# Where q is turned in mixer B, which PSUM banks its pools get, and when the last norm's products are issued: a three-part change to a hybrid encoder trunk

## The chip, the core and the metric

The kernel runs on one core of one Trainium2 chip. The metric is device microseconds (us) of one execution. The names used for the engines are: PE for TensorE's matrix products, PEld for its weight loads, ACT for ScalarE, DVE for VectorE, POOL for GpSimd, SP for SyncE, which issues most transfers. Each engine takes its instructions in program order.

## The reference, cut to what matters

The trunk has two layers on 1024 tokens of width 1024. Layer 0 uses mixer A (neighbourhood attention on a grid), layer 1 mixer B. Each layer then adds a gated embedding, and one RMS norm ends the trunk.

```python
def mixer_b(h, w_in, q_norm_g, k_norm_g, w_out):
    # h: (1, 1024, 1024); 16 query heads, 4 key/value heads, head size 64
    proj = h @ w_in
    q, k, v, gate = jnp.split(proj, [1024, 1024 + 256, 1024 + 512], axis=-1)
    q = rms_norm(heads(q, 16), q_norm_g)
    k = rms_norm(heads(k, 4), k_norm_g)
    q, k = axial_rope(q), axial_rope(k)
    # four query heads share one key/value head
    sc = einsum('bkgqd,bksd->bkgqs', q_block, k) * scale
    pr = softmax(sc)
    o = einsum('bkgqs,bksd->bkgqd', pr, v)
    return (o * silu(gate)) @ w_out

def reference(x, p, ...):
    for i in range(2):
        h = rms_norm(x, norm_g[i])
        x = x + (mixer_a if i == 0 else mixer_b)(h, ...)
        g = sigmoid(rms_norm(x, ple_norm_g[i]) @ ple_w_gate[i])
        x = x + g * (p[i] @ ple_w_proj[i])
    return rms_norm(x, final_norm_g)
```

## The kernel before

Each operand of a product is split into a high part (rounded to the fp32r format) and a low part (the rest), and a product is the sum of three PE passes: high by high, high by low, low by high. A name that ends in `h` or `A` is a high part, one that ends in `l` or `B` a low one.

The kernel runs in stages: mixer A, `dense_phase(0)` (output projection of layer 0 and its gated embedding), mixer B (from about 707 to 1340 us), and `dense_phase(1)` (the same for layer 1, and the last norm). The order of the instructions on each engine is the order in which the code writes them; semaphores that the framework derives from tiles and their buffers do the rest.

Mixer B's attention is a list of 128 steps `n`, each for a query head `h`, a half `hf` of the tokens and a block `t` of 128 queries. One step has these parts:

- `f_S`: four PE products `s<-KA,QS` and `s<-KB,QS` put the scores of 128 queries against 1024 keys into a tile `s` of two PSUM banks, and DVE takes a row minimum `mn<-s` (L1211).
- `f_E`: ACT computes `P<-s,mn`, the exponential (L1217).
- `f_T`: eight PE transposes `t<-ident,P` (L1227) fill two PSUM tiles of the pool `psT`, which has two buffers; ACT copies each to `PTh` (L1229), and DVE subtracts for `PTl` (L1230). A psT buffer is free for its next user only after these readers.
- `f_AV`, once for two steps: eight products `o<-PTh,V` and then eight `o<-PTl,V`.

`q_stack` makes the queries of the heads that come next: four PE transposes `t<-ident,qt` (L1181) into one more psT tile, an ACT copy `th<-t` (L1183), and then, some ticks later, the high and low parts `QS<-th` on ACT (L1190) and DVE (L1191). It runs 16 times, 15 of them in the attention.

`mix(att, dense)` interleaves this list with projections that fill PE (`dense` items: `d<-wh,HTh` and its kind; they make the gate, the next q, k and v), one item whenever the share of work done says so. In it a queued call of `q_stack` waits in `after`, an `Evac` list, and is run after the next dense item.

[...] In mixer B the pools were opened in the order `pd` (one bank, bank 0), `psS` (scores, banks 1 to 4), `psT` (5 and 6), `psO` (7). At mixer B's entry `dalloc` and `qalloc` hand out `pd` and `psO` in turn for the first projections. What `dense_phase(1)` allocates takes these banks over afterwards: its first product tile `Y[0]` lies in bank 0.

In `dense_phase(1)` the last norm needs `X*gain` for one half of the columns; POOL makes it, tile after tile (L1706), after ACT has squared the tile (L1701).

Of the kernel before, what the change touches and what calls it, by code (L numbers as in the profile page):

```python
# [11 lines left out]
F32 = mybir.dt.float32  # L12
# [6 lines left out]
PSUM = bass.MemoryType.PSUM  # L19
# [18 lines left out]
DT = (5, 2)  # L38
FIN = (4, 4)
HOLD = 2  # L40
WARM = (8, 8)
THIRDS = {0: ((0, 1, 2), (0, 2, 1)), 1: ((0, 1, 2), (0, 1, 2))}
DP = 1
# [115 lines left out]
def trunk(ctx, tc, x, wts, rpb, gains, hgains, mask, rope, gain0, out):  # L159
# [156 lines left out]
    def mm(ps, a, b, first, last):  # L316
        pe.matmul(ps, a, b, start=first, stop=last, skip_group_check=True)  # L317
# [41 lines left out]
            while self.left:  # L359
                self.left.pop(0)()  # L360

    leave, after = Evac(), Evac()
    after.wait = True

    def mix(att, dense, lead=0, hold=0):
        for f, _ in dense[:lead]:
            f()
            pulse()
        kept = dense[len(dense) - hold:]
        dense = list(dense[lead:len(dense) - hold])  # L370
        total = sum(c for _, c in dense)
        span = sum(c for _, c in att)
        spent = done = 0.0
        since = True
        for i, (f, c) in enumerate(att):
            kind = getattr(f, "kind", None)
            if kind == "apart" and not since and (dense or len(kept) > 2):
                d, e = (dense or kept).pop(0)
                d()
                spent += e  # L380
                after.run()
            if kind in ("apart", "blocks"):
                since = False
            f()
            leave.run()
            pulse()
            done += c
            while dense and spent < total * done / span - 1e-6:
                leave.run()
                leave.wait = i + 1 < len(att) and getattr(att[i + 1][0], "first", False)  # L390
                d, c = dense.pop(0)
                d()
                leave.wait = False
                spent += c
                since = True
                after.run()
        leave.run()
        after.run()
        for f, _ in dense + kept:
            f()  # L400
            pulse()
# [598 lines left out]
    def mixer_b(pend):  # L1000
        with ExitStack() as es:
# [2 lines left out]
            kp = es.enter_context(tc.tile_pool(name="kp", bufs=3))  # L1004
            one = es.enter_context(tc.tile_pool(name="bone", bufs=1))
            sb = es.enter_context(tc.tile_pool(name="bsb", bufs=2))
            pd = es.enter_context(tc.tile_pool(name="bpd", bufs=1, space=PSUM))
            psS = es.enter_context(tc.tile_pool(name="bps", bufs=2, space=PSUM))
            psT = es.enter_context(tc.tile_pool(name="bpt", bufs=2, space=PSUM))
            psO = es.enter_context(tc.tile_pool(name="bpo", bufs=1, space=PSUM))  # L1010

# [3 lines left out]
            def dalloc():  # L1015
                if pro[0]:
                    pro[1] += 1
                    if pro[1] % 2 == 0:
                        return psO.tile([128, 512], F32, name="o")
                return pd.tile([128, 512], F32, name="d")  # L1020

            gg, ylive = {}, {}
            KA, KB, V, QT, QST, P, RS, OP = {}, {}, {}, {}, {}, {}, {}, {}
            later = Later()

            pro = [False, 0]

            def qalloc():
                pro[1] += 1
                if pro[0] and pro[1] % 2 == 0:  # L1030
                    return psO.tile([128, 512], F32, name="o")[:, :256]
                return pd.tile([128, 512], F32, name="d")[:, :256]

            def rope_in(dst, raw, tab, eng):
                nh = raw.shape[1] // 64
# [140 lines left out]
            def q_stack(pair, hf):  # L1176
                g = pair // 2
                ps = psT.tile([128, 4, 128], F32, name="t")
                c = slice((pair % 2) * 128, (pair % 2) * 128 + 128)
                for t in range(4):  # L1180
                    pe.transpose(ps[:, t], QT[g, hf][:, t, c], ident)  # L1181
                raw = sb.tile([128, 512], F32, name="th")
                act.activation(raw, ps.rearrange("p t c -> p (t c)"), AF.Copy)  # L1183
                for j in range(2):
                    own, oth = slice(64 * j, 64 * j + 64), slice(64 - 64 * j, 128 - 64 * j)
                    qs = sb.tile([128, 512], F32R, name="QS", bufs=3)
                    QST[2 * pair + j, hf] = qs

                    def high(qs=qs, own=own, oth=oth):
                        act.activation(qs[own], raw[own], AF.Copy)  # L1190
                        post.add(DQ, lambda: dve.tensor_tensor(qs[oth], raw[own], qs[own], ALU.subtract))  # L1191
                    if pro[0]:
                        high()
                    else:
                        post.add(QO[j], high)
# [39 lines left out]
            def f_AV(h, hf, t):  # L1235
                if t == 1:
                    OP[h, hf] = psO.tile([128, 512], F32, name="o")
                o = OP[h, hf][:, (t - 1) * 128:(t + 1) * 128]
                for k in range(NT):
                    mm(o, V[h // 4][:, k], PTh[:, k], t == 1 and k == 0, False)  # L1240
                for k in range(NT):
                    mm(o, V[h // 4][:, k], PTl[:, k], False, t == 3 and k == NT - 1)
                if t == 3:
                    fin = head_end(sb, h, hf, RS[h, hf], OP.pop((h, hf)), ylive, 1, gg, talloc)
                    if fin:
                        later.add(FIN[1], fin)
# [29 lines left out]
            for g in range(4):  # L1276
                att = []
                for n in range(32 * g, 32 * g + 32):
                    h, hf, t = steps[n]
                    av = n >= 2 and n % 2 == 0  # L1280
                    w = CB if av else CN
                    def turn():
                        if WQ.gate:
                            WQ.gate = False
                        later.tick()
                    att.append((turn, w[0]))
                    if av:
                        att.append((lambda n=n: f_AV(*steps[n - 1]), w[1]))
                    te = [(blocks(n), w[2])]
                    if n + 1 < len(steps):  # L1290
                        te.append((exps(n + 1), w[3]))
                    if n % 2 == 0 and n > 0:
                        te.reverse()
                    att += te
                    if n + 2 < len(steps):
                        def scores(n=n):
                            f_S(*steps[n + 2])
                            WQ.gate = n % 2 == 1 if n < 112 else None
                        att.append((scores, w[4]))
                    m = n + QS_AT  # L1300
                    if m % 8 == 0 and m < len(steps):
                        hn, fn, _ = steps[m]
                        att.append((lambda hn=hn, fn=fn: after(lambda: q_stack(hn // 2, fn)), 0.0))
                    if YLOAD_B <= n < YLOAD_B + NT:
                        att.append((lambda t=n - YLOAD_B: load_y(1, t), 0.0))
                if g == 3:
                    att.append((lambda: f_AV(*steps[-1]), CB[1]))
                def gates(p):
                    return [i for hf in range(2) for i in gate_items("bg", p, hf, dalloc, sb, gg)]
                dense = []  # L1310
                if g > 0:
                    dense += left
                if g < 3:
                    qi = q_items(g + 1, pool)
                    kv = kv_items(1, pool) if g == 1 else [None, None]
                    dense += kv[:-2] + qi[:KS] + [k for k in kv[-2:-1] if k] + qi[KS:8] + [k for k in kv[-1:] if k] + gates(2 * g + 1) + qi[8:]
                    left = gates(2 * g + 2)
                else:
                    WQ.cap[3] = 2
                    dense += gates(2 * g + 1) + pp_items(1, dalloc, sb, TAGS_B)  # L1320
                mix(att, dense, hold=HOLD + 1 if g == 3 else 0)
# [185 lines left out]
    def dense_phase(l):  # L1507
        with ExitStack() as es:
# [9 lines left out]
            pend = []  # L1518
# [83 lines left out]
            for kind in ("ple",):  # L1602
                final = l == 1
                sq = sb.tile([128, 2, NT], F32, name="sq")
                due = []
                gt = g2
                for hf in range(2):
# [69 lines left out]
                    for t, i in order:  # L1677
# [22 lines left out]
                        if hf == 0:  # L1700
                            act.activation(junk[:, cs], X[t][:, cs], AF.Square, accum_out=sq[:, 0, t:t + 1])  # L1701
                            if final:
                                due.append(t)
                            while due and n >= 17:
                                u = due.pop(0)
                                pool.tensor_tensor(X[u][:, cs], X[u][:, cs], gt[:, cs], ALU.mult)  # L1706
                            continue
# [70 lines left out]
```

## Time and profile before

| | |
|---|---|
| median of 3 runs | 1526.33 us (1525.96 to 1526.63) |
| the profiled execution | 1525.28 us, of which its span is 1523.4 us |
| granted TensorE clock | 0.997 |
| PE busy | 1496.9 us, 98% of the span |
| DVE, ACT, POOL busy | 1096.4 us (72%), 899.8 us (59%), 303.8 us (20%) |
| PE's products of mixer B's q turns (L1181) | 64 transposes, 10.1 us busy |
| ACT's copies of them (L1183) | 16, 9.4 us busy |

A row of a timeline has the start in us from the start of the span, the duration, the engine, the line of the code, the operation, the tiles it writes and reads (`out<-in`), and in brackets the idle time of the engine just before it with what ended it. Several like instructions in a row are one row (`x4`). A row of groups ends with busy time and mean ns of one, and then the idle time ahead of the group. Matmuls overlap: the next begins before the last one's end, so PE's time is best read from start to start.

### The profile page before, as it was taken

The page shows a single profiled execution, that of the slowest core. Times are in us where ns is not written, and L with a number is a line of the kernel's source. Part 1 is how long each engine was busy: PE and PEld are TensorE (multiplying, and loading weights), DVE is VectorE, ACT ScalarE, POOL GpSimd, SP SyncE. Part 2 cuts the span into 40 slices and gives each one's busy share as a digit, 9 for nine tenths or more (in the row PEclk, how much of TensorE's full clock was granted, in tenths as well). Part 3 has the DMA queues.
Part 4 walks back from the last instruction along what each step waited for, and adds up shares of the span by engine and source line. Part 5 has one row for each costly group of instructions (what it writes and reads, how often), then busy time and mean ns, then how long its engine had stood idle before and what let it go on. Part 6 is the DMA issues. An engine that isn't in the chain of part 4 may idle for free.

```text
span 1523.4 us, 24376 instructions
## 1 busy us (share of the span) xinstructions
PE 1496.9 (98%) x8976; PEld 1314.9 (86%) x8976; DVE 1096.4 (72%) x2091; ACT 899.8 (59%) x1801; POOL 303.8 (20%) x413
## 2 busy tenths in 40 slices
PE   8999999999999999999999999999999999999997
PEld 8888988988988888888998999989999888878786
DVE  7566576377477599767888786777877777789856
ACT  6565465366466635443467776666767777744432
POOL 1222232133112000010222222443131300000022
PEclk9999999999999999999999999999999999999999
DMA  8325255263121963262210111111111122763123
GB/s 255 120 98 139 82 144 163 63 157 93 36 87 56 345 249 97 83 196 93 75 50 22 32 45 50 40 32 54 47 31 45 38 76 68 237 228 115 66 88 134
DMA packets 91096, 157.22 MB, mean 103 GB/s; under 512 B 18144, under 2 KB 54112, under 8 KB 90464
## 3 DMA queue, kind: packets, MB, share of 16 engines
q1 hardware_dynamic: 85824, 139.66, 27.9%
q0 software_dynamic: 2560, 8.39, 3.1%
q10 hardware_dynamic: 2592, 7.61, 1.4%
q8 instruction: 71, 1.16, 0.3%
q14 instruction: 49, 0.40, 0.1%
HBM read 125.10 MB, written 50.83 MB: 115 GB/s over the span
## 4 chain that ended last, share of the span: by engine, by line
PE 43%; DVE 6%; ACT 2%; issue 1%; DMA 0%; POOL 0%; ACTq 0%; DVEq 0%; POOLq 0%
PE d L317 19%; PE o L317 9%; PE s L317 7%; PE t L1227 7%; PE t L317 1%; DVE xn L1560 1%; DVE PTl L1230 1%; DVE X L1456 0%; PE t L1181 0%; DVE wl L231 0%; DVE mn L1211 0%; DVE HTl L482 0%; DVE HTl L1402 0%; ACT PTh L1229 0%; ACT th L1183 0%
## 5 line engine op out<-in xcount | busy, mean ns | idle before, releaser
L317 PE MATMUL d<-wh,HTh 128*128 128x256 f32 (+1 forms) x1032 | 342.5, 334 | 3.9 <-ACT HTh L481 1.6
L317 PE MATMUL d<-wh,HTl 128*128 128x256 f32 (+1 forms) x1032 | 338.0, 329 | 0.3 <-DVE HTl L482 0.3
L317 PE MATMUL d<-wl,HTh 128*128 128x256 f32 (+1 forms) x1032 | 336.7, 328 | 0.0
L1230 DVE TENSOR_TENSOR PTl<-t,PTh 128x512 fp32r<-128x512 f32 x256 | 165.1, 684 | 108.7 <-ACT PTh L1229 107.5
L317 PEld LDWEIGHTS d<-wh,HTh 128*128 128x128 f32 x1032 | 194.8, 190 | 24.5 <-ACT HTh L481 2.0
L317 PEld LDWEIGHTS d<-wl,HTh 128*128 128x128 f32 x1032 | 194.7, 190 | 19.3
L317 PEld LDWEIGHTS d<-wh,HTl 128*128 128x128 f32 x1032 | 194.9, 190 | 18.8 <-DVE HTl L482 0.5
L317 PE MATMUL d<-HTh,wh 128*128 128x512 f32 x504 | 205.2, 407 | 0.0
L317 PE MATMUL d<-HTh,wl 128*128 128x512 f32 x504 | 198.2, 393 | 0.0
L317 PE MATMUL d<-HTl,wh 128*128 128x512 f32 x504 | 197.3, 392 | 0.0
L1217 ACT ACTIVATE P<-s,mn 128x1024 f32<-128x1024 f32 x128 | 142.8, 1116 | 51.8 <-DVE mn L1211 50.9
L1229 ACT ACTIVATE PTh<-t 128x512 fp32r<-128x512 f32 x256 | 139.9, 594 | 52.8 <-PE t L1227 52.0
L1211 DVE TENSOR_REDUCE mn<-s 128x1 f32<-128x1024 f32 x128 | 154.7, 1209 | 11.2 <-PE s L317 11.0
L1227 PE MATMUL t<-ident,P 128*128 128x128 f32 x1024 | 136.4, 274 | 5.2 <-ACT th L1183 2.9
L317 PE MATMUL s<-KA,QS 128*128 128x512 f32 (+2 forms) x384 | 134.5, 404 | 0.0
L1227 PEld LDWEIGHTS t<-ident,P 128*128 128x128 f32 x1024 | 115.2, 140 | 16.6 <-DVE PTl L1230 6.7
L231 DVE TENSOR_TENSOR wl<-wstage,wh 128x1024 fp32r<-128x1024 f32 x78 | 100.3, 1290 | 34.9 <-ACT wh L226 34.4
L317 PE MATMUL s<-KB,QS 128*128 128x512 f32 (+2 forms) x384 | 121.6, 371 | 0.0
L775 DVE TENSOR_TENSOR PTl<-t,PTh 128x384 fp32r<-128x384 f32 (+1 forms) x128 | 66.6, 520 | 75.4 <-ACT PTh L774 74.0
L317 PE MATMUL o<-PTh,V 128*128 128x256 f32 (+2 forms) x672 | 118.5, 287 | 1.2 <-DVE Y L496 0.8
L317 PE MATMUL o<-PTl,V 128*128 128x256 f32 (+2 forms) x672 | 119.1, 288 | 0.7 <-DVE PTl L1230 0.6
L317 PEld LDWEIGHTS d<-HTh,wl 128*128 128x128 f32 x504 | 94.6, 188 | 21.7
(237 smaller groups left out, 2694.1 us busy)
## 6 DMA issues: line engine op xcount, KB each, us to landing
wstage<-in_wts SPq DMA_DIRECT2D x88, 512.0 KB
pp<-ppD SPq DMA_DIRECT2D x32, 256.0 KB
X<-in_x SPq DMA_DIRECT2D x15, 512.0 KB
rb<-rD SPq DMA_DIRECT2D x56, 128.0 KB
ppD<-th SPq DMA_DIRECT2D x20, 256.0 KB
tD0t<-in_wts SPq DMA_DIRECT2D x16, 256.0 KB
tD1t<-in_wts SPq DMA_DIRECT2D x16, 256.0 KB
xD<-X SPq DMA_DIRECT2D x8, 512.0 KB
```

Of the source, the lines that this page charges most:

```text
L231: eng.tensor_tensor(lo[:, c:c + n], s[:, c:c + n], hi[:, c:c + n], ALU.subtract)
L317: pe.matmul(ps, a, b, start=first, stop=last, skip_group_check=True)
L775: dve.tensor_tensor(PTl[:, sl], ps[:, :m], PTh[:, sl], ALU.subtract)
L1211: dve.tensor_reduce(mn, ps, axis=AX.X, op=ALU.min)
L1217: act.activation(p, ps, AF.Exp, bias=mn, scale=-1.0, accum_out=RS[h, hf][:, t:t + 1])
L1227: pe.transpose(ps[:, i], p[:, k * 128:(k + 1) * 128], ident)
L1229: act.activation(PTh[:, ks, c], ps, AF.Copy)
L1230: dve.tensor_tensor(PTl[:, ks, c], ps, PTh[:, ks, c], ALU.subtract)
L1560: dve.scalar_tensor_tensor(xn, X[t], rn[m][:, i:i + 1], g1, op0=ALU.mult, op1=ALU.mult)
```

## The change

It has three parts.

1. `q_stack` no longer goes through `after`. A queued call is kept in `turned` and run by the next `f_AV`, between its eight products with `PTh` and its eight with `PTl`. `after` is gone from `mix`.
2. The pool `psS` is opened ahead of `pd`: the scores have banks 0 to 3 now, `pd` has bank 4, psT and psO stay. At the entry of mixer B the first eight tiles of the projections (`ENTRY`) lie in the first half of scores tiles, and those behind them in `pd` and `psO` in turn; `qalloc` follows `dalloc`.
3. The products `X*gain` of the last norm are written into the program when the list `pend` of transposes is empty, not from `n >= 17` on.

```diff
-    leave, after = Evac(), Evac()
-    after.wait = True
+    leave = Evac()
...
                 d()
                 spent += e
-                after.run()
...
-                after.run()
         leave.run()
-        after.run()
...
+            psS = es.enter_context(tc.tile_pool(name="bps", bufs=2, space=PSUM))
             pd = es.enter_context(tc.tile_pool(name="bpd", bufs=1, space=PSUM))
-            psS = es.enter_context(tc.tile_pool(name="bps", bufs=2, space=PSUM))
...
                 if pro[0]:
                     pro[1] += 1
+                    if pro[1] <= ENTRY:
+                        return psS.tile([128, 1024], F32, name="s")[:, :512]
                     if pro[1] % 2 == 0:
                         return psO.tile([128, 512], F32, name="o")
...
             def qalloc():
-                pro[1] += 1
-                if pro[0] and pro[1] % 2 == 0:
-                    return psO.tile([128, 512], F32, name="o")[:, :256]
-                return pd.tile([128, 512], F32, name="d")[:, :256]
+                return dalloc()[:, :256]
...
                     mm(o, V[h // 4][:, k], PTh[:, k], t == 1 and k == 0, False)
+                while turned:
+                    turned.pop(0)()
                 for k in range(NT):
...
-                        att.append((lambda hn=hn, fn=fn: after(lambda: q_stack(hn // 2, fn)), 0.0))
+                        att.append((lambda hn=hn, fn=fn: turned.append(lambda: q_stack(hn // 2, fn)), 0.0))
...
-                            while due and n >= 17:
+                            while due and not pend:
```

The lines of the code move by a few: L1181, L1183, L1217, L1227 and L1229 of before are L1178, L1180, L1214, L1224 and L1226 in the changed kernel, L317 is L318, and L1706 is L1705.

PE's order at one of the 15 places, which the profile of before has at 1112 to 1118 us (ten of the 15 are of this kind). `o<-PTh,V` and `o<-PTl,V` are the products with v, `t<-ident,qt` turns q, `t<-ident,P` turns the exponentials; the rows left out are products `d<-wh,HTh` and their kind. Before:

```order
L317 MATMUL o<-PTh,V 128x256 x8
L317 MATMUL o<-PTl,V 128x256 x8
L1227 MATMUL t<-ident,P 128x128 x8
L317 MATMUL s<-KA,QS 128x512 x2
L317 MATMUL s<-KB,QS 128x512 x2
...
L317 MATMUL d<-wh_11748,HTl 128x256
L1181 MATMUL t<-ident,qt 128x128 x4
L1227 MATMUL t<-ident,P 128x128 x8
```

and in the changed kernel:

```order
L318 MATMUL o<-PTh,V 128x256 x8
L1178 MATMUL t<-ident,qt 128x128 x4
L318 MATMUL o<-PTl,V 128x256 x8
L1224 MATMUL t<-ident,P 128x128 x8
L318 MATMUL s<-KA,QS 128x512 x2
L318 MATMUL s<-KB,QS 128x512 x2
...
L318 MATMUL d<-wh_11748,HTl 128x256
L1224 MATMUL t<-ident,P 128x128 x8
```

Between the turn of q and the next turn of exponentials there were no instructions; now eight products stand there, and the turn of q comes one step earlier. At the other five places q's turn stood just ahead of `o<-PTh,V`, and moves behind it.

ACT's order at the same place. `P,rs<-s,mn` is the exponential, `th<-t` the copy of q's psT tile, `PTh<-t` the copies of the exponentials' tiles, `qt<-d` and `t<-qt` work for a later q. Before:

```order
L1093 ACTIVATE qt<-d 128x256
L1057 ACTIVATE t_12306<-qt 128x256
L1229 ACTIVATE PTh<-t 128x4x128 x2
L1217 ACTIVATE P,rs<-s,mn 128x1024 x2
L1229 ACTIVATE PTh<-t 128x4x128 x2
L532 ACTIVATE Y<-o 64x512
L1093 ACTIVATE qt<-d 128x256
L1057 ACTIVATE t_12412<-qt 128x256
L1183 ACTIVATE th<-t 128x512
L1229 ACTIVATE PTh<-t 128x4x128 x2
```

and in the changed kernel:

```order
L1090 ACTIVATE qt<-d 128x256
L1054 ACTIVATE t_12306<-qt 128x256
L1226 ACTIVATE PTh<-t 128x4x128 x2
L1214 ACTIVATE P,rs<-s,mn 128x1024
L1180 ACTIVATE th<-t 128x512
L1214 ACTIVATE P,rs<-s,mn 128x1024
L1226 ACTIVATE PTh<-t 128x4x128 x2
L529 ACTIVATE Y<-o 64x512
```

The copy of q's tile stood directly ahead of the copies of the next exponentials' tiles, and stands between two exponentials now.

PE's order at the end of mixer B and the first product of `dense_phase(1)` (`d<-wh_13753,HTh`), with the semaphores that an instruction waits for. Before:

```order
L317 MATMUL d<-wh_13662,KA 128x512
L317 MATMUL d<-wl_13663,KA 128x512
L317 MATMUL d<-wh_13662,KB 128x512
L317 MATMUL d<-wh_13753,HTh 128x512 [waits DMAHW6_49,Activation_49]
L317 MATMUL d<-wl_13754,HTh 128x512
```

and in the changed kernel:

```order
L318 MATMUL d<-wh_13662,KA 128x512
L318 MATMUL d<-wl_13663,KA 128x512
L318 MATMUL d<-wh_13662,KB 128x512
L318 MATMUL d<-wh_13753,HTh 128x512 [waits DMAHW6_49]
L318 MATMUL d<-wl_13754,HTh 128x512
```

With `pd` in bank 4, the tile in bank 0 that `dense_phase(1)` fills first has a scores tile ahead of it, not the last `pd` tile, and the wait for ACT's copy of that one is gone from its first product; the next product tile in bank 4 has it now.

POOL's order and SP's order are the same before and after, in every row: the eight products of part 3 stand where they stood, and each waits for what it waited for.

More of the change, by code (lines that the diff above doesn't have):

```diff
@@ L40 @@
 HOLD = 2
+ENTRY = 8
 WARM = (8, 8)
@@ L1024, in mixer_b @@
             later = Later()
+            turned = []
             pro = [False, 0]
             def qalloc():
-                pro[1] += 1
-                if pro[0] and pro[1] % 2 == 0:
-                    return psO.tile([128, 512], F32, name="o")[:, :256]
-                return pd.tile([128, 512], F32, name="d")[:, :256]
+                return dalloc()[:, :256]
             def rope_in(dst, raw, tab, eng):
```

## The prediction

> **What bounds the kernel now.** I read the page first: its span, each engine's busy time, and the chain that ended last.
>
> ```profile
> span 1523.4 us, 24376 instructions
> PE 1496.9 (98%) x8976; PEld 1314.9 (86%) x8976; DVE 1096.4 (72%) x2091; ACT 899.8 (59%) x1801; POOL 303.8 (20%) x413
> PE 43%; DVE 6%; ACT 2%; issue 1%; DMA 0%; POOL 0%; ACTq 0%; DVEq 0%; POOLq 0%
> ```
>
> PE is the bound. The change adds and removes no product, so it can only win what PE stands still: 26.5 us by this page, of which only the places that the change touches count. So I read next what PE waited for.
>
> ```profile
> PE t L1227 <- ACT th L1183: 2.9, 7, 0.8
> PE t L1227 <- DVE PTl L1230: 1.8, 3, 0.9
> ...
> PE t L480 <- DVE HTl L482: 1.7, 2, 1.5
> ...
> PE d L317 <- ACT th L619: 0.7, 1, 0.7
> ...
> PE d L317 <- ACT th L1149: 0.6, 1, 0.6
> ...
> PE d L317 <- ACT th L1617: 0.3, 1, 0.3
> PE t L1181 <- DVE PTl L1230: 0.2, 1, 0.2
> ```
>
> The columns are total, times and longest. The first row is the largest, and it is what part 1 changes: seven times the turn of the exponentials stood until ACT had copied q's psT tile. The timeline of one of the seven shows how.
>
> ```profile
> 1112.88 1.12 PE L317 MATMUL o<-PTl,V 128*128 128x256 f32 x8
> 1113.02 1.12 ACT L1217 ACTIVATE P<-s,mn 128x1024 f32<-128x1024 f32 x1 [1.23 <-DVE mn L1211]
> ...
> 1113.84 1.04 PE L1227 MATMUL t<-ident,P 128*128 128x128 f32 x8
> ...
> 1114.47 1.09 ACT L1229 ACTIVATE PTh<-t 128x512 fp32r<-128x512 f32 x2 [0.25 <-PE t L1227]
> ...
> 1115.10 1.29 DVE L1230 TENSOR_TENSOR PTl<-t,PTh 128x512 fp32r<-128x512 f32 x2 [2.12 <-ACT PTh L1229]
> ...
> 1117.07 0.60 PE L1181 MATMUL t<-ident,qt 128*128 128x128 f32 x4
> ...
> 1117.51 0.60 PE L1227 MATMUL t<-ident,P 128*128 128x128 f32 x4
> ...
> 1118.01 0.58 ACT L1183 ACTIVATE th<-t 128x512 f32<-128x512 f32 x1
> ...
> 1118.64 0.66 PE L1227 MATMUL t<-ident,P 128*128 128x128 f32 x4 [0.54 <-ACT th L1183]
> ```
>
> psT has two buffers. At 1117.07 q takes one, the first four turns of P take the other at 1117.51, and the second four need q's again, which ACT frees at 1118.59.
>
> **Part 1, what it wins.** Four transposes take 0.44 us from start to start (1117.07 to 1117.51), so the second four would have begun at 1117.95, not at 1118.64: 0.69 us, and they then took 0.66 instead of 0.60: 0.75 us lost, where the wait shows 0.54. The difference of 0.21 is the overlap with the four before, which the wait's number leaves out. Seven waits: 2.9 + 7 x 0.21 = 4.4 us. In the new order q's tile is filled at about 1112.88, and the next user of its buffer is the second half of the P turns, 0.96 us of products and 0.44 of transposes later, about 1114.72. Its copy starts 0.64 after the turn (at 1113.52, by the distance of 819.93 and 820.57 below) and ends at 1114.10. So the wait is gone with 0.6 us to spare, and I take all seven.
>
> Two times q's own turn was late, for a buffer that DVE had not yet read out:
>
> ```profile
> 1003.39 0.28 PE L317 MATMUL d<-wh,HTl 128*128 128x256 f32 x1
> ...
> 1003.72 0.66 PE L1181 MATMUL t<-ident,qt 128*128 128x128 f32 x4
> ...
> 1287.35 0.39 PE L317 MATMUL d<-wl,KA 128*128 128x512 f32 x1
> ...
> 1287.57 0.40 PE L317 MATMUL d<-wh,KB 128*128 128x512 f32 x1
> ...
> 1288.20 0.66 PE L1181 MATMUL t<-ident,qt 128*128 128x128 f32 x4 [0.23 <-DVE PTl L1230]
> ```
>
> A product of 256 columns takes 0.12 from start to start (eight from 1112.88 to 1113.84) and one of 512 takes 0.22 (1287.35 to 1287.57), so these turns were 0.21 and 0.41 late and ran 0.06 longer each: 0.7 us. In the new order q comes right behind `o<-PTh,V`, when both psT buffers have long been read: gone as well.
>
> **Part 1, what it costs.** At the other five places q's turn moves behind the eight products, by 0.96 us, and ACT's copy with it. The exponential stands behind the copy on ACT:
>
> ```profile
> 819.93 0.60 PE L1181 MATMUL t<-ident,qt 128*128 128x128 f32 x4
> 820.29 1.19 PE L317 MATMUL o<-PTh,V 128*128 128x256 f32 x8
> 820.57 0.60 ACT L1183 ACTIVATE th<-t 128x512 f32<-128x512 f32 x1 [0.97 <-PE t L1181]
> 821.06 1.11 ACT L1217 ACTIVATE P<-s,mn 128x1024 f32<-128x1024 f32 x1
> ...
> 822.97 1.09 ACT L1229 ACTIVATE PTh<-t 128x512 fp32r<-128x512 f32 x2 [0.71 <-PE t L1227]
> ...
> 832.55 0.42 PEld L1227 LDWEIGHTS t<-ident,P 128*128 128x128 f32 x4 [0.44 <-DVE PTl L1230]
> ```
>
> The exponential moves from 821.06 to 822.02 and ends at 823.13, where the copy of P's tile stood ready at 822.97: `PTh` is 0.15 us later. PE doesn't wait for it there, but ten us on PE waits for DVE's `PTl` (the last row), and DVE has little slack until then, so I count 0.15 on PE. At most four of the five places run into such a wait; with nothing absorbed and my 0.15 doubled it is 1.2 us, with all absorbed 0; I take 0.5. At the ten places the copy now stands ahead of an exponential too: at 1113.02 that one would start at 1114.01. It delays `PTh` from 1114.47 to about 1115.11 and the end of the `PTl` pair from 1116.39 to 1117.03, but the second half of the next P turns needs that buffer only at 1117.95. Cost nothing, covered by 0.9 us; were that cover gone, see the rival below.
>
> **Part 2.** At the entry, the first product waits for the last tanh (`th L1617`, 0.3) and the third tile of the projections for ACT's copy (`th L1149`, 0.6). Eight scores tiles are still two buffers in turn, as `pd` and `psO` were, and in the order both waits stand on the same instructions. I take 0. With 0.21 each they are worth 1.3 at most; a loss isn't in sight, since the scores tiles are needed only after the projections. At the exit it does change a wait, by where the banks fall:
>
> ```profile
> 1339.63 0.39 PE L317 MATMUL d<-wh,KB 128*128 128x512 f32 x1
> 1340.10 0.60 ACT L619 ACTIVATE th<-d 128x512 f32<-128x512 f32 x1 [1.81 <-PE d L317]
> ...
> 1340.75 0.50 PE L317 MATMUL d<-wh,HTh 128*128 128x512 f32 x1 [0.74 <-ACT th L619]
> ```
>
> The first product of `dense_phase(1)` waited for ACT to empty bank 0. In the new order it doesn't, and the next user of that bank comes a whole product tile later. It would begin at 1339.85 instead of 1340.75, and last 0.39 instead of 0.50: 1.0 us. What might hold it next is its data, `HTh`, or its weights; both were there earlier, since its only other wait is a transfer that shows no stall here. From 0 to 1.0; I take 1.0.
>
> **Part 3.** POOL's order and waits are the same in both programs. Nothing moves: 0.
>
> **The sum.** 4.4 + 0.7 - 0.5 + 1.0 = 5.6 us from the profiled execution (1525.28 us, span 1523.4), which would be 1519.7 with a span of 1517.8. It lies 1.05 under the median of the runs, so the median would go from 1526.33 to 1520.7.
>
> **The rivals.** B: half of part 1's gain is given back. DVE and ACT set the pace between these places:
>
> ```profile
> 823.00:833.00 10.00, 9.99 (x63) 8.51 (x61) 8.85 (x13) 8.51 (x16) 0.00 (x0) 1.00 0.15 44
> ```
>
> The columns are PE, PEld, DVE, ACT and POOL busy. DVE has 1.15 us of these 10 left. Where PE comes earlier and DVE doesn't, PE waits later at the next P turn, as it did three times for `PTl` (1.8 us above). For it speaks this row; against it, that the seven places lie in stretches with slack (2.12 idle ahead of DVE's `PTl` at 1115.10). Half of 5.1, and 1.2 instead of 0.5 lost, leaves 2.55 - 1.2 + 1.0 = 2.4: 1523.9.
>
> C: the collision in `dense_phase(1)` goes as well. While POOL's products ran, DVE's instructions got longer:
>
> ```profile
> 1430.23 2.47 DVE L1560 SCALAR_TENSOR_TENSOR xn<-X,rn,gain 128x1024 f32<-128x1024 f32 x2
> 1432.62 0.68 DVE L1618 SCALAR_TENSOR_TENSOR th<-th,pp 128x512 f32<-128x512 f32 x1
> ...
> 1434.86 1.31 POOL L1706 TENSOR_TENSOR X<-X,gain 128x512 f32<-128x512 f32 x1 [149.39 <-ACT junk L1701]
> ...
> 1435.31 1.41 DVE L1618 SCALAR_TENSOR_TENSOR th<-th,pp 128x512 f32<-128x512 f32 x1 [1.28 <-ACT th L1617]
> ...
> 1437.36 3.53 DVE L1560 SCALAR_TENSOR_TENSOR xn<-X,rn,gain 128x1024 f32<-128x1024 f32 x2
> ...
> 1438.34 1.47 POOL L1706 TENSOR_TENSOR X<-X,gain 128x512 f32<-128x512 f32 x1 [2.17 <-ACT junk L1701]
> ```
>
> 0.73 and 1.06 us longer, and PE waited for DVE's `HTl L482` just behind (1.5 at the longest). If the products came later, 1.7 us more would be won: 1519.0. Against it stands that the order on POOL is the same. [...]
>
> D, the other side: ACT takes its queue in order, and q's copy stands ahead of an exponential at 15 places, delaying it by 0.96 to 0.99. If all of it reached PE, it would be 15 x 0.99 = 14.9 lost against 6.1 won: 1535.1. It decides from 6.1 / 15 = 0.41 us a place (no change), and slower by over 0.2% from 0.61. The margins above (0.9 us; 0.15 over) speak against it. [...]
>
> That the change doesn't do what it says is part of the forecast: the entry and the norm's products are taken as unmoved.
>
> **How the numbers follow.** Forecast 0.64 (its own range 1519.9 to 1522.3: sum 4.0 to 6.4 for a loss of 0 to 1.2 and an exit of 0.2 to 1.0), B 0.19, C 0.09, D 0.04, else 0.04. 0.2% is 3.05 us, about what a measurement can tell from no change: faster is under 1523.28. The forecast and C lie there, and a third of B: 0.64 + 0.09 + 0.06 = 0.79. Slower is D and little else: 0.04. The rest, 0.17, is the same. The range goes from C to B's price, 1519.0 to 1524.0, which leaves out D, what is beyond B, and some of C.
>
> **What the next profile would show.** Right: the wait of L1227 for q's copy gone from the list of PE's waits (2.9 to under 0.3), none of `d L317` for `th L619`, PE idle by some 4 to 5 us less, and mixer B ending about 4.6 us earlier; POOL's products still behind each square, and the long DVE rows of 1435 to 1441 still there. Wrong: PE waits for `PTl` at P turns of over 3 us in total (B), or for q's copy at the P turn that now follows it 0.96 us later (D).

## The result and the profile after

The changed kernel took 1518.25 us (median of 6 executions, 1517.36 to 1519.44) against 1526.13 before (6 executions, 1524.20 to 1526.63): a ratio of 0.9951, 95% interval 0.9938 to 0.9964. That is 7.9 us faster. The forecast was 5.6 us faster, 1520.7 us, and the time lies 0.75 us under the lower end of the range. Measured again in two later sessions, each on one chip with the kernel before, the same change was worth 5.8 and 5.7 us. So there are two questions: whether the mechanism was right, and what the other 2 us were.

The page of the changed kernel, its span and busy times (the chain is that of before, PE 43%, in every figure):

```profile
span 1516.6 us, 24373 instructions
PE 1492.6 (98%) x8976; PEld 1312.5 (87%) x8976; DVE 1100.0 (73%) x2091; ACT 898.4 (59%) x1801; POOL 303.9 (20%) x413
```

This execution took 1518.46 us. What PE waited for in it (total, times, longest):

```profile
PE t L1224 <- DVE PTl L1227: 2.0, 3, 0.9
PE t L477 <- DVE HTl L479: 1.7, 2, 1.5
...
PE s L318 <- ACT th L1146: 0.6, 1, 0.6
...
PE t L1224 <- ACT th L1113: 0.5, 2, 0.3
...
PE s L318 <- ACT th L1616: 0.2, 1, 0.2
```

The wait of the P turns for q's copy (2.9, seven times) is gone, and so are q's own wait for `PTl` and the wait of `d` for `th L619`. The entry's two waits are where they were, on a scores tile `s` now in place of `d`. The timeline shows the place that the prediction showed:

```profile
1109.59 1.12 PE L318 MATMUL o<-PTh,V 128*128 128x256 f32 x8
1110.55 0.60 PE L1178 MATMUL t<-ident,qt 128*128 128x128 f32 x4
1110.90 1.20 PE L318 MATMUL o<-PTl,V 128*128 128x256 f32 x8
1111.94 1.04 PE L1224 MATMUL t<-ident,P 128*128 128x128 f32 x8
...
1111.18 0.60 ACT L1180 ACTIVATE th<-t 128x512 f32<-128x512 f32 x1 [1.73 <-PE t L1178]
1111.68 1.11 ACT L1214 ACTIVATE P<-s,mn 128x1024 f32<-128x1024 f32 x1
...
1112.77 1.09 ACT L1226 ACTIVATE PTh<-t 128x512 fp32r<-128x512 f32 x2
...
1115.17 1.03 PE L1224 MATMUL t<-ident,P 128*128 128x128 f32 x8
```

q's copy starts 0.63 us after its turn and is done at 1111.78, 0.6 us ahead of the second half of the P turns (1112.38). Both P turns run in one piece (1.04 and 1.03 for eight). The exponential waits behind the copy, as the prediction had it: DVE's minimum for it is there at 1110.66 (`mn`, L1208, 1109.44 and 1.22), and ACT, idle until q's turn lets the copy start at 1111.18, begins it at 1111.68. The length of the attention can be read from the first and the last P turn, whichever way the execution began:

```profile
L1227 PE MATMUL t<-ident,P x1024: 270/272/329, 774.4 to 1333.4; 128*128 128x128 f32 x171
...
L1224 PE MATMUL t<-ident,P x1024: 270/272/332, 773.5 to 1327.6; 128*128 128x128 f32 x171
```

559.0 us before (L1227), 554.1 after (L1224): 4.9 us. And the exit, in the changed kernel:

```profile
1333.79 0.39 PE L318 MATMUL d<-wh,KB 128*128 128x512 f32 x1
1334.01 0.39 PE L318 MATMUL d<-wh,HTh 128*128 128x512 f32 x1
...
1334.26 0.60 ACT L616 ACTIVATE th<-d 128x512 f32<-128x512 f32 x1 [1.81 <-PE d L318]
```

The first product of `dense_phase(1)` starts 0.22 us behind the one ahead of it, before ACT has begun to empty bank 4; before, it was 1.12. From the first P turn to the last product of PE the two profiles are 5.95 us apart (740.87 and 734.92). The spans are 6.8 apart: 0.9 us more, and these lie ahead of 100 us, where both programs are alike.

### The profile page after: what moved, and what is told of

It is laid out like the page before. It is cut to its first block, busy times and chain, and to the rows that moved or that the text cites. A ratio compares the mean times of both kernels' runs of the same rounds, so it can differ in the third digit from the quotient of the medians.

```text
span 1516.6 us, 24373 instructions
## 1 busy us (share of the span) xinstructions
PE 1492.6 (98%) x8976; PEld 1312.5 (87%) x8976; DVE 1100.0 (73%) x2091; ACT 898.4 (59%) x1801; POOL 303.9 (20%) x413
## 4 chain that ended last, share of the span: by engine, by line
PE 43%; DVE 6%; ACT 2%; issue 1%; DMA 0%; POOL 0%; ACTq 0%; DVEq 0%; POOLq 0%
PE d L318 19%; PE s L318 8%; PE o L318 8%; PE t L1224 7%; PE t L318 1%; DVE xn L1559 1%; DVE PTl L1227 1%; DVE X L1455 0%; DVE mn L1208 0%; PE t L1178 0%; DVE wl L232 0%; DVE HTl L479 0%; DVE HTl L1401 0%; ACT wh L227 0%; ACT P L1214 0%
## 5 line engine op out<-in xcount | busy, mean ns | idle before, releaser
L318 PE MATMUL d<-wh,HTh 128*128 128x256 f32 (+1 forms) x1000 | 332.6, 335 | 3.0 <-ACT HTh L478 2.2
L318 PE MATMUL d<-wh,HTl 128*128 128x256 f32 (+1 forms) x1000 | 328.5, 330 | 0.3 <-DVE HTl L479 0.3
L318 PE MATMUL d<-wl,HTh 128*128 128x256 f32 (+1 forms) x1000 | 327.7, 330 | 0.0
L1227 DVE TENSOR_TENSOR PTl<-t,PTh 128x512 fp32r<-128x512 f32 x256 | 164.6, 684 | 106.8 <-ACT PTh L1226 106.4
L318 PEld LDWEIGHTS d<-wh,HTh 128*128 128x128 f32 x1000 | 188.2, 189 | 22.8 <-ACT HTh L478 2.5
L318 PE MATMUL d<-HTh,wh 128*128 128x512 f32 x504 | 205.2, 407 | 0.0
L318 PEld LDWEIGHTS d<-wl,HTh 128*128 128x128 f32 x1000 | 188.5, 189 | 19.3
L318 PEld LDWEIGHTS d<-wh,HTl 128*128 128x128 f32 x1000 | 188.3, 189 | 18.8 <-DVE HTl L479 0.5
L318 PE MATMUL d<-HTh,wl 128*128 128x512 f32 x504 | 198.1, 393 | 0.0
L318 PE MATMUL d<-HTl,wh 128*128 128x512 f32 x504 | 197.3, 392 | 0.0
L1214 ACT ACTIVATE P<-s,mn 128x1024 f32<-128x1024 f32 x128 | 142.9, 1117 | 47.2 <-DVE mn L1208 46.2
L1226 ACT ACTIVATE PTh<-t 128x512 fp32r<-128x512 f32 x256 | 139.4, 595 | 45.8 <-PE t L1224 45.4
L1208 DVE TENSOR_REDUCE mn<-s 128x1 f32<-128x1024 f32 x128 | 155.0, 1211 | 9.4 <-PE s L318 8.8
L1224 PE MATMUL t<-ident,P 128*128 128x128 f32 x1024 | 135.0, 273 | 2.5 <-DVE PTl L1227 2.0
L318 PE MATMUL s<-KA,QS 128*128 128x512 f32 (+2 forms) x384 | 134.3, 404 | 0.0
L1224 PEld LDWEIGHTS t<-ident,P 128*128 128x128 f32 x1024 | 115.5, 140 | 12.9 <-DVE PTl L1227 6.9
L318 PE MATMUL s<-KB,QS 128*128 128x512 f32 (+2 forms) x384 | 121.6, 370 | 0.0
L318 PE MATMUL o<-PTl,V 128*128 128x256 f32 (+2 forms) x672 | 120.3, 290 | 0.7 <-DVE PTl L1227 0.6
L318 PE MATMUL o<-PTh,V 128*128 128x256 f32 (+2 forms) x672 | 118.1, 287 | 1.2 <-DVE Y L493 0.8
L318 PEld LDWEIGHTS d<-HTh,wl 128*128 128x128 f32 x504 | 94.6, 188 | 21.6
```

Source lines behind the costliest of these rows:

```text
L1208: dve.tensor_reduce(mn, ps, axis=AX.X, op=ALU.min)
L1214: act.activation(p, ps, AF.Exp, bias=mn, scale=-1.0, accum_out=RS[h, hf][:, t:t + 1])
L1224: pe.transpose(ps[:, i], p[:, k * 128:(k + 1) * 128], ident)
L1226: act.activation(PTh[:, ks, c], ps, AF.Copy)
L1227: dve.tensor_tensor(PTl[:, ks, c], ps, PTh[:, ks, c], ALU.subtract)
```

## The experiments

Two theories stood against each other for the 2 us: S, that the change is worth what the profile shows from mixer B on and the rest is spread between executions, and E or T, that a part is worth more than the sum gave it.

**One part at a time.** Part 1 alone is the edit of `mix`, `f_AV` and `turned`:

```diff
-att.append((lambda hn=hn, fn=fn: after(lambda: q_stack(hn // 2, fn)), 0.0))
+att.append((lambda hn=hn, fn=fn: turned.append(lambda: q_stack(hn // 2, fn)), 0.0))
...
+                while turned:
+                    turned.pop(0)()
```

> Part 1 alone: q's turn between the products with PTh and PTl, the banks, the entry and the norm's products as before. Theory S (the change is worth what the profile after shows from mixer B on, 5.9 us, and the rest of the 7.9 is spread between executions): 4.9 us faster, about 1521.2, the seven waits for q's copy gone, the wait of 0.7 for th L619 at the first product of dense_phase(1) still there. Theory T (part 1 is worth more than its sum, because copies and exponentials come earlier downstream): 6.5 or more. Theory E (entry or norm products act): 4.9 here, and the missing 2 us in one of the next two runs.

Measured: 1519.47 us (1519.23 to 1521.02) against 1525.02 (21 executions), ratio 0.9965, interval 0.9952 to 0.9977: 5.55 us faster. The length of the attention and the waits that stay:

```profile
L1224 PE MATMUL t<-ident,P x1024: 270/272/332, 774.8 to 1329.2; 128*128 128x128 f32 x171
...
PE d L317 <- ACT th L615: 0.7, 1, 0.7
```

554.4 us, 4.6 less than before, and the exit's wait of 0.7 is still there. Part 2 alone:

```diff
+psS = es.enter_context(tc.tile_pool(name="bps", bufs=2, space=PSUM))
 pd = es.enter_context(tc.tile_pool(name="bpd", bufs=1, space=PSUM))
-psS = es.enter_context(tc.tile_pool(name="bps", bufs=2, space=PSUM))
...
+                    if pro[1] <= ENTRY:
+                        return psS.tile([128, 1024], F32, name="s")[:, :512]
...
```

with `qalloc` following `dalloc` as in the change.

> Part 2 alone: scores' banks first and the entry's tiles in scores banks; q is turned where it was. Theory S: 1.0 us faster, 1525.1, all of it at the first product of dense_phase(1); the waits for th L1617 and th L1149 at the entry stay at 0.3 and 0.6. Theory E: 2 to 3 us faster, and the part above 1.0 shows as shorter waits between 707 and 760 us. Theory T: 1.0.

Measured: 1523.53 us (1522.10 to 1526.58, 11 executions), ratio 0.9991, interval 0.9982 to 1.0: 1.5 us faster by the medians, though the interval reaches up to no change; the profile from the first P turn to the last product shows 0.9 (739.99 against 740.87). The entry's waits are as they were:

```profile
PE s L318 <- ACT th L1149: 0.6, 1, 0.6
...
PE s L318 <- ACT th L1617: 0.2, 1, 0.2
```

Part 3 alone:

```diff
-while due and n >= 17:
+while due and not pend:
```

> Part 3 alone: the last norm's products are written into the program when the list of transposes is empty. Theories S and T: no change, within 1 us of before, POOL's rows at 1434.9 and 1438.3 and DVE's long rows behind them as before. Theory E: 1 to 2 us faster, DVE's pair at 1437 down from 3.5 to 2.5 us.

Measured: 1524.80 us (1523.63 to 1526.22, 11 executions), ratio 0.9998, interval 0.9989 to 1.0007: no change. POOL's two products and DVE's pair between them, in this run:

```profile
1434.65 1.30 POOL L1706 TENSOR_TENSOR X<-X,gain 128x512 f32<-128x512 f32 x1 [149.75 <-ACT junk L1701]
...
1437.15 3.52 DVE L1560 SCALAR_TENSOR_TENSOR xn<-X,rn,gain 128x1024 f32<-128x1024 f32 x2
...
1438.12 1.46 POOL L1706 TENSOR_TENSOR X<-X,gain 128x512 f32<-128x512 f32 x1 [2.17 <-ACT junk L1701]
```

The collision stands as before. The whole change beside its parts:

> The whole change once more, beside its parts on the same chip. Theory S: 6 to 6.5 us faster, the sum of the three runs within 1 us, and a start (up to 100 us) that differs between the profiles by up to 1 us with no order in it. Theories T and E: 7.5 to 8 again.

Measured: 1519.18 us (1517.47 to 1519.97, 5 executions), ratio 0.9959, interval 0.9946 to 0.9973: 5.84 us faster. From the first P turn to the last product 734.74 us. The parts by the same stretch sum to 4.6 + 0.9 - 0.2 = 5.3, the whole is 6.1 here and 5.95 in the first comparison; by the medians the parts sum to 7.3 and the whole is 5.8. So the sum missed its "within 1 us" by the medians, and what the difference is no run shows. The main claim of S holds: the 7.9 didn't come again.

**Where the rest was: the start.** In all profiles the first PE instruction starts at 1.35 us and the last turn of X, the end of the first norm's transposes, anywhere from 37.0 to 39.5; from there to the first P turn it takes 735.3 to 736.5 in all but one program (the one with the pools' order alone, below). The windows from 6 to 20 us tell most of why. First the kernel before, then the changed kernel in the first comparison, then the same changed kernel in the last session (columns as in the prediction, then PEclk, DMA's share and GB/s):

```profile
6.00:20.00 14.00, 12.09 (x75) 11.41 (x74) 10.50 (x25) 9.69 (x19) 2.80 (x4) 0.88 1.00 364
...
6.00:20.00 14.00, 10.79 (x83) 9.46 (x82) 11.32 (x27) 10.50 (x20) 2.83 (x4) 1.00 1.00 366
...
6.00:20.00 14.00, 10.69 (x74) 10.18 (x73) 10.28 (x25) 9.32 (x18) 2.81 (x4) 0.88 1.00 370
```

The granted clock of PE is 0.88 there in nine of the 14 profiles, 0.76 in one (the latest start, 39.5), and 1.00 in four. Those four have the four earliest starts, 37.0 to 37.8. It isn't a property of the program: the changed kernel shows 1.00 once and 0.88 twice. Over all timed executions that list a clock, those of the kernel before at a mean clock of 0.999 took 1524.01 us on average (16) and those below 1525.27 (39); of the changed kernel 1517.76 (4) and 1519.16 (12). At like clocks the change is worth 6.25 and 6.12 us. This mean sorts the executions only roughly: it also holds a fall behind the last product, which costs nothing (0.50 from 1518.32 us on in the profile of before, whose last product ends at 1515.29), so that the 1.3 us between the groups are the start's alone isn't shown.

The last session ran the changed kernel once more:

> The changed kernel again, beside the run above on one chip. Theory S: 5.8 to 6.3 us faster than before on this chip; from the first turn of P to the last product 734.8 us within 0.3, as in its two other profiles, while the start, up to the last turn of X, lies anywhere from 37.8 to 39.5 us.

Measured: 1519.14 us (1518.46 to 1519.40, 5 executions) against 1524.82 (15), ratio 0.9962, interval 0.9950 to 0.9975: 5.7 us faster; the stretch from the first P turn was 735.03, the start 38.8.

**How far q's turn may move.** Three kernels are the changed one with q's turn at another place. Behind all the products:

```diff
-                while turned:
-                    turned.pop(0)()
                 for k in range(NT):
                     mm(o, V[h // 4][:, k], PTl[:, k], False, t == 3 and k == NT - 1)
+                while turned:
+                    turned.pop(0)()
```

> The changed kernel with one edit: q's turn stands behind all eight products with PTl, directly ahead of the turns of P. Theory distance (what counts is the PE work between q's turn and the second half of the P turns, against the 1.27 us until ACT has emptied q's tile): 0.88 us of work stands there now, so the second half waits 0.39 us and fills 0.06 longer, at 15 places: 6.8 us slower than the changed kernel, about 1525, and PE's list shows some 15 waits of L1224 for th L1180. Rival (the early place in ACT's queue is what counts): no such waits, the time of the changed kernel within 1 us.

Measured: 1527.57 us (1526.04 to 1528.09, 10 executions), 8.4 us slower than the changed kernel and slower than before (ratio 1.0017, interval 1.0007 to 1.0026). The wait is back, at 13 places, and PTl's grew too:

```profile
PE t L1224 <- ACT th L1180: 3.4, 13, 0.3
PE t L1224 <- DVE PTl L1227: 2.5, 7, 0.9
```

13 x (3.4/13 + 0.21) = 6.1 us for the copy alone, by the reckoning of the prediction. Behind four of the eight products with `PTl`:

```diff
                     mm(o, V[h // 4][:, k], PTl[:, k], False, t == 3 and k == NT - 1)
+                    while turned and k == 3:
+                        turned.pop(0)()
```

> The changed kernel with one edit: q's turn stands behind the first four of the eight products with PTl. Theory distance: 0.44 + 0.48 + 0.44 = 1.36 us of work against 1.27 us, so no wait is left, and the time is that of the changed kernel within 0.7 us. If the copy takes longer to free its tile than I reckon: up to 15 short waits of 0.1 to 0.2 us, 1.5 to 3 us slower.

Measured: 1520.73 us (1520.03 to 1522.65, 8 executions), and the length of the attention with PE's waits for ACT and DVE:

```profile
L1224 PE MATMUL t<-ident,P x1024: 269/273/330, 774.0 to 1330.4; 128*128 128x128 f32 x171
...
PE t L1224 <- DVE PTl L1227: 2.7, 7, 0.9
...
PE t L1224 <- ACT th L1113: 0.9, 2, 0.7
...
832.96 1.25 PE L1224 MATMUL t<-ident,P 128*128 128x128 f32 x8 [0.25 <-DVE PTl L1227]
...
916.23 1.03 PE L1224 MATMUL t<-ident,P 128*128 128x128 f32 x8
```

The distance was enough, as expected: no wait for q's copy. But the attention is 556.4 us, 2.3 longer than in the changed kernel (554.1). The wait for `PTl` comes seven times, not three. That is rival D: the exponential stands behind the copy, 0.48 us later than in the changed kernel, and now PE feels it, at four of the five places where q's turn stood ahead of `o<-PTh,V`: the P turn at 916.23, behind these four, comes 142.3 us after the first one, and its like in the kernel before (914.91) and in the changed kernel (914.06) 140.5. That is 1.8 of the 2.3 us, 0.44 a place. The expectation missed this second limit. On the other side, behind four of the eight products with `PTh`:

```diff
                     mm(o, V[h // 4][:, k], PTh[:, k], t == 1 and k == 0, False)
+                    while turned and k == 3:
+                        turned.pop(0)()
```

> The changed kernel with one edit: q's turn stands behind the first four of the eight products with PTh, 0.48 us earlier. Theory two-sided (too late an exponential costs on the one side, too short a distance to the P turns on the other; the changed kernel's place is just inside both): the time of the changed kernel within 0.5 us, no wait for th L1180, PTl waits of PE as in the changed kernel (2.0). Rival (each 0.48 us that the copy comes earlier wins what it lost when it came later): 1 to 2.5 us faster than the changed kernel.

Measured: 1517.91 us (1517.03 to 1519.35, 4 executions), and the attention:

```profile
L1224 PE MATMUL t<-ident,P x1024: 270/272/329, 773.6 to 1327.4; 128*128 128x128 f32 x171
```

553.8 us against 554.1, 553.8 and 554.2 in the three profiles of the changed kernel: nothing won by being earlier. (Its profiled execution had a start at a clock of 1.00, as the changed kernel's first one had, so the times of few executions don't decide here.)

**Which half of part 2.** The order of the two pools without the entry's tiles in scores banks:

> The kernel before with the order of the two PSUM pools alone, without the entry's tiles in scores banks. Theory S: the whole gain of part 2, from the last turn of P to the last product 181.9 becomes 180.9 us, and the entry's waits for th L1617 and th L1149 stay: 1.0 us faster than before. Rival (the entry's tiles are what helps): no gain.

Measured: 1526.81 us (1524.61 to 1528.38, 10 executions), ratio 1.0013, interval 1.0003 to 1.0022: slower than before. Theory S missed. The rival was right that the entry's tiles matter, but neither expected a loss. The exit's gain is there (180.9 us from the last P turn on), and the entry lost 3.3 us (739.0 from the last turn of X to the first P turn, against 735.7):

```profile
705.72 0.60 PE L480 MATMUL t<-ident,xn 128*128 128x128 f32 x4
...
707.88 0.68 DVE L482 TENSOR_TENSOR HTl<-t,HTh 128x512 fp32r<-128x512 f32 x1
...
708.62 0.38 PE L317 MATMUL d<-wh,HTh 128*128 128x256 f32 x1 [2.31 <-DVE HTl L482]
...
709.50:712.90 3.40, 3.40 (x18) 3.40 (x18) 3.12 (x10) 0.00 (x0) 0.00 (x0) 0.50 0.17 69
712.90:720.00 7.10, 6.58 (x55) 6.34 (x55) 1.91 (x6) 2.15 (x9) 0.00 (x0) 1.00 0.07 21
```

`pd` is in bank 4 now, and there the stage before has its last transposes, which ACT and then DVE read out (the row at 707.88). Mixer B's first product waits for that, 2.3 us (0.25 in the kernel before, for `th L1617`), and 0.9 us after the restart PE's granted clock falls to 0.50 for 3.4 us, by an estimate from these two another 1.7 us. So the entry's tiles are no ornament: beside the new order of the pools they take the place that `pd` lost. Beside the old order they should do nothing, since their banks are free as early as bank 0; no run has them alone.

**Two waits that the change left.** POOL's first two products behind the third, which has to wait for its own tile:

```diff
-while due and not pend:
-    u = due.pop(0)
+while due and seq.index(t) >= 2:
+    u = due.pop()
```

> The changed kernel with one edit: POOL's first two products of the last norm stand behind the third, which waits for its own tile, so all three run some 12 us later than now; the other five as before. Theory collision (DVE's pair at L1559 and its L1617 lose 1.7 us to POOL's products, and PE waits 1.7 us for what follows them): DVE's pair back to 2.5 us, L1617 there back to 0.7, PE's longest wait for HTl L479 down from 1.5 to under 0.3 us: 1.7 us faster than the changed kernel. Rival (DVE is late there for another reason, or the three products now collide with L232): less than 0.5 us.

Measured: 1517.17 us (1516.70 to 1517.33, 5 executions), ratio to before 0.9950, interval 0.9938 to 0.9963; about 2 us faster than the changed kernel's 1519.1 (median of all 16 executions), 1.75 by the profile from the last P turn on (179.1 against 180.9).

```profile
1429.12 0.69 DVE L1617 SCALAR_TENSOR_TENSOR th<-th,pp 128x512 f32<-128x512 f32 x1 [1.28 <-ACT th L1616]
...
1430.46 2.48 DVE L1559 SCALAR_TENSOR_TENSOR xn<-X,rn,gain 128x1024 f32<-128x1024 f32 x2
...
1440.85 5.25 POOL L1705 TENSOR_TENSOR X<-X,gain 128x512 f32<-128x512 f32 x3 [160.59 <-ACT junk L1700]
...
1443.17 1.78 DVE L1617 SCALAR_TENSOR_TENSOR th<-th,pp 128x512 f32<-128x512 f32 x1
1444.98 1.67 DVE L1618 SCALAR_TENSOR_TENSOR X<-th,X 128x512 f32<-128x512 f32 x1
...
PE t L477 <- DVE HTl L479: 0.2, 1, 0.2
```

DVE's instructions are back to 0.69 and 2.48, and PE's wait for `HTl` there is gone. The collision has moved to 1443 us (1.78 and 1.67 in place of 0.69 each), where PE doesn't wait for DVE. This is what rival C priced at 1.7 us. The condition of part 3 doesn't move these products; this edit does.

k's two turns between the products as well:

```diff
-items.append((lambda hf=hf: k_stack(i, st["raw"], hf), 450.0))
+def turn_k(hf=hf):
+    if pro[0]:
+        k_stack(i, st["raw"], hf)
+    else:
+        turned.append(lambda: k_stack(i, st["raw"], hf))
+items.append((turn_k, 450.0))
```

> The changed kernel with one edit: k's two turns (L1110) in the attention go between the products with PTh and PTl too, one of them next to a turn of q. Theory distance: the two waits of L1224 for th L1113 (0.3 and 0.2 shown, 0.47 each from start to start) are gone, 0.9 us faster than the changed kernel. Rival (two copies ahead of one exponential are too much): PE waits for PTl or the copy at that place, no gain or up to 0.5 us lost.

Measured: 1518.55 us (1517.23 to 1519.19, 5 executions): 0.6 us faster than the changed kernel by the median, which five executions can't tell from none, and 0.6 to 0.9 by the profiles (734.13 against 734.74, 734.92 and 735.03), so the expected 0.9 is at the upper end. The waits for `th L1113` are gone, and one for the gate's tile came:

```profile
PE d L318 <- ACT G L585: 0.5, 1, 0.5
```

Both together:

> The changed kernel with k's turns between the products too and POOL's first two products of the last norm behind the third. If both gains of the single edits add: 0.6 and 1.75 us by the profiles, 2.3 us faster than the changed kernel beside it, about 1516.7.

Measured: 1515.76 us (1515.22 to 1516.93, 5 executions), ratio to before 0.9942, interval 0.9929 to 0.9954; beside the changed kernel in that session (1519.14) 3.4 us faster, 2.7 by the profile from the first P turn on (732.29 against 735.03). It is the fastest of all.

## Why the prediction was right or wrong, point by point

- **The base and the range: wrong.** The step "the median would go from 1526.33 to 1520.7" set the sum against the median of three executions. The kernel before took 1524.84 us by the median of 55 later ones, 1.5 less, and they lie up to 3.3 us apart (1523.37 to 1526.65). From that base the same sum gives 1519.2; the changed kernel took 1519.1 by the median of all its 16 executions. The other 0.9 us down to 1518.25 are the six of the first comparison, which lie that much under the 16. The range was built from the terms of the sum and the rivals, and had no term for this spread: with one of 1.5 us on either side it would have held 1518.25. Why the kernel before was slower in its first executions than later stays open; neither their clocks nor their chip are listed. One bound of the forecast's own range is also mis-added: its terms (5.1 less a loss of 0 to 1.2, and an exit of 0.2 to 1.0) give 4.1 to 6.1, not 4.0 to 6.4.
- **The gain: right, a little low.** 5.6 forecast, 5.8 and 5.7 by the two later comparisons, 6.1 to 6.25 at like clocks, 5.8 to 6.1 by three profiles from the first P turn on. One sign missed: PE's idle time fell by 2.5 us (26.5 to 24.0), not by 4 to 5. The forecast was a sum of times from start to start, and part of these shows as PE's busy time, as its 0.21 us a wait does; and the changed kernel's profile waits 0.6 us longer for `HTh` at its start.
- **The seven waits (4.4) and q's own two (0.7): right.** All gone. With each start of PE's instructions in the one profile set against the same one's in the other, the seven places gained 4.2 us and the two 0.5. The correction of 0.21 us a wait carried it: by the waits' own numbers the seven would have been 2.9.
- **The cost at five places (0.5): wrong in size, 0 measured.** The first step held: `PTh` begins 0.83 us behind its P turns, not 0.70: late by 0.13 (0.15 forecast). What followed was absorbed, as these rows of the changed kernel show:

```profile
820.66 0.60 ACT L1180 ACTIVATE th<-t 128x512 f32<-128x512 f32 x1 [1.94 <-PE t L1178]
...
821.41 1.03 PE L1224 MATMUL t<-ident,P 128*128 128x128 f32 x8
...
822.24 1.09 ACT L1226 ACTIVATE PTh<-t 128x512 fp32r<-128x512 f32 x2
...
825.21 1.09 ACT L1226 ACTIVATE PTh<-t 128x512 fp32r<-128x512 f32 x2 [0.74 <-PE t L1224]
...
914.06 1.03 PE L1224 MATMUL t<-ident,P 128*128 128x128 f32 x8
```

  At the next `PTh` ACT still waited 0.74 us for PE, so the delay had ended on ACT. On DVE, `PTl` began 1.47 us behind its P turn (1.33 before), and the next one 1.30 behind its own (1.27 before), so there too it was all but gone. And PE lost nothing: from the first P turn to the one at 914.06, behind four of the five places, it took 140.5 us, as before:

```profile
914.91 1.04 PE L1227 MATMUL t<-ident,P 128*128 128x128 f32 x8
```

  So the step "DVE has little slack until then, so I count 0.15 on PE" failed: the slack was enough for 0.13 us. That the term is real further on shows the kernel with the turn four products later: there `PTl` is still 0.5 us late at the second P turn, and 0.48 us cost 2.3.
- **Part 2: net right (1.0 at the exit, measured 0.9 to 1.0), by a reason with a hole.** "I take 0" for the entry held for both edits together; that the new order of the pools alone would put the first product behind DVE in bank 4, I hadn't looked for.
- **Part 3: right,** 0 by its own run.
- **Rivals.** B didn't come: PE waited 2.0 us for `PTl` in place of 1.8. C's price was right and its condition not met. DVE's instruction at 1435.31 took 0.73 us more than its like beside a product of POOL of which 0.86 us were left when it began (1434.86 and 1.31, less 1435.31). D's mechanism is there, and begins to cost between 0 and 0.48 us behind the place that the change took.

## What to carry to other kernels

A turn through a shared buffer had two limits here: enough work of PE between it and the buffer's next user to cover the reader (directly ahead of the P turns it cost 8.4 us), and a place in the reader's queue that doesn't make the main chain late (four products behind the change's place, 2.3 us); try a place on either side before a place is called good. When pools change banks, look at who held the new bank at the stage's entry and who gets the old one at its exit. For effects of some us, compare like stretches of two profiles, and read the clock at the start before two times are subtracted.

## What the runs showed of the hardware

After a wait of 2.3 us PE's granted clock fell to 0.50 for 3.4 us in the kernel with the pools' order alone (709.5 to 712.9), beginning 0.9 us after PE had work again: products of 256 columns were 0.21 us apart there (709.60, 709.82 and 710.03), and 0.12 just ahead (708.84 and 708.96). A wait of 1.55 us for `HTl L479` in the changed kernel left the clock at 1.00 in the windows around it (1433 to 1440). At the start PE waits for its first `HTh`, 1.3 to 2.8 us in the eleven profiles that were read for it, and from 6 to 20 us the clock was below full in ten of 14 profiles (0.88 in nine, 0.76 in one) and full in four. Three of the four have waits of 1.3, 1.4 and 2.24 us, and three of the ten have 1.4, 1.5 and 1.58, so the length alone doesn't decide it.

Nor does PE's busy time ahead of it. One stretch each of the kernel with the pools' order alone, of the kernel before and of the changed kernel (columns as above):

```profile
705.00:709.00 4.00, 1.70 (x11) 1.26 (x10) 2.15 (x4) 1.81 (x4) 0.00 (x0) 1.00 0.06 24
...
9.63:13.05 3.42, 1.84 (x13) 1.64 (x14) 3.00 (x9) 3.39 (x7) 0.71 (x2) 1.00 1.03 422
...
9.59:13.00 3.41, 2.14 (x16) 1.94 (x16) 3.03 (x8) 3.35 (x8) 1.01 (x2) 1.00 1.02 419
```

The first is the one ahead of the 0.50 from 709.5 on. Behind the second the clock was 0.50 from 13.05 to 16.46 and 1.00 after it; behind the third it stayed at 1.00 (13.00 to 16.41). But it stayed at 1.00 also behind 1.86 us of work in the 3.41 us from 1432.95 on in the changed kernel, around the wait for `HTl L479`, which is about the second's 1.84. What decides it isn't shown. Nor is this all of the start's spread: in the kernel before eight turns of X took 1.91 us at 7.39, where no clock is on record yet (the first is at 9.63), and 1.06 at 22.23.

DVE and POOL: while POOL's products ran, DVE's `th<-th,pp` took 1.41 us (1435.31 in the kernel before) in place of 0.68 (1432.62) and the pair `xn` 3.53 (1437.36) in place of 2.47 (1430.23); with the products moved away 0.69 and 2.48.

Order: in the profile of the kernel before, PE's 8976 products, ACT's 1469 activations, DVE's 2091 instructions and POOL's 413 start in the order in which the program has their lines.
